# A two-layer hybrid decoder trunk on one core: four plain pairs a feed-forward block instead of five, and other places for operands, squares and bias

## The chip, the core and the metric

The kernel runs on one core of a Trainium2 chip. The core has five engines with an instruction queue each: TensorE (PE, with its weight loads shown as PEld), VectorE (DVE), ScalarE (ACT), GpSimd (POOL) and SyncE (SP), which here only issues DMAs. An engine works through its own instructions in order and waits on semaphores for the others. The metric is the device time of one execution in microseconds; the median of the runs is compared.

## The reference

The input is one sequence of 512 positions with 1024 features. Two layers follow, each a feed-forward block, a mixer of three branches (a state-space scan, attention in a window of 128, a gated unit), and a second feed-forward block. All is in float32.

```
for l in range(DEPTH):
    x = x + 0.5 * swiglu(rmsnorm(x, ffn1_norm[l]), ffn1_w_gate[l], ffn1_w_up[l], ffn1_w_down[l])
    h = rmsnorm(x, mix_norm[l])
    ...
    x = x + jnp.concatenate([y_ssd, y_att, y_sgu], axis=-1) @ w_out[l]
    x = x + 0.5 * swiglu(rmsnorm(x, ffn2_norm[l]), ffn2_w_gate[l], ffn2_w_up[l], ffn2_w_down[l])
return rmsnorm(x, final_norm)

def swiglu(x, w_gate, w_up, w_down):
    return (jax.nn.silu(x @ w_gate) * (x @ w_up)) @ w_down
```

The hidden width of a feed-forward block is 2816, which is 22 chunks of 128. The change touches the two first products of the feed-forward blocks, `x @ w_gate` and `x @ w_up`, the sum of squares of the norms, and the place in which the relative bias of the attention is made.

## The kernel before

The residual x is kept transposed on the chip, as eight tiles `xT` of 128 features by 512 positions. Each float32 product is made of three products in a shorter format: an operand is split into a high part (a cast on ScalarE) and a low part (a subtraction on VectorE), and high times high, low times high and high times low are added up in PSUM. `split` (line 135) does this for a weight tile `raw` of 128x1024 and gives `whi` and `wlo`; `split_x` (line 150) does it for a chunk of x, which it also multiplies with the weight of the norm, and gives `xhi` and `xlo`. `raw` has five buffers, `whi` and `wlo` have four each.

There are four feed-forward blocks; they are called F1 to F4 in order of time here, and between F1 and F2, and between F3 and F4, lies a mixer.

The norm is applied late. `Stat` (line 175) squares the eight chunks on ScalarE and adds the squares up, by default on GpSimd. TensorE adds over the partitions (line 194), VectorE and GpSimd make the reciprocal root, TensorE spreads it (line 207), and VectorE copies it to the tile R (line 371 in a feed-forward block). Products with weights go on meanwhile; only what leaves PSUM is multiplied with R.

A feed-forward block makes its 22 pairs of a gate chunk and an up chunk in two ways. The first `HEAD` pairs (line 42: five) are plain: `in_products` (line 227) runs two tiles of 24 matmuls of 512 columns for each pair, and `emit` (line 354) takes them out of PSUM. A gate tile n (even) is multiplied with R and goes through Silu on ScalarE; an up tile n (odd) is multiplied with it and gives one tile of `h`. Up to three tiles wait for R before the first is taken out.

The other pairs are made by a scheme of seven products of half the size in place of eight (`Seven` and the loop at line 441): sums of weight quarters are multiplied with sums of x quarters, in 84 matmuls of 256 columns. For this x times norm weight times R is needed explicitly, with four sums for each of four pairs of chunks. `operands(c)` (line 335) makes them: two products on VectorE into a temporary (line 343), four sums (lines 346 to 349), then `parts`: one cast of 128x1792 on ScalarE (line 126) and one subtraction on VectorE (line 127). The results are the tiles `as0` to `as3`. The first block of a seven-product pair (line 448) reads all four of them. The temporary is `temp()`, with the tag T and one buffer, so each `operands` waits until line 127 of the one before has read it. The weight sums of a seven-product pair (lines 383 to 386) use the same buffer.

`operands(0)` to `operands(3)` are called in `emit` behind the gate tiles 2, 4, 6 and 8.

In F1 a part of the mixer's work is done too: `attention_bias` (line 97) multiplies the bias table with a one-hot matrix on TensorE (line 106), copies the result to a buffer (line 108) and writes it to DRAM by DMAs of GpSimd's queue (line 109), in four turns over two buffers. It is called when two tiles of `h` are there, and its buffers are parts of one `temp()`.

The code is written in program order; the framework that builds the kernel then orders the instructions of each engine by its own schedule, except where the code asks for the order as written (F1's opening, line 284). The order of the engines shown below is that of the built program.

Of the kernel before, what the change touches and what calls it, by code (L numbers as in the profile page):

```python
# [19 lines left out]
F32 = mybir.dt.float32  # L20
# [6 lines left out]
P = 128  # L27
D = 1024
KD = D // P
T = 512  # L30
# [8 lines left out]

COLS = ("ffn1_norm", "mix_norm", "ffn2_norm", "ssd_norm", "attn_out_norm", "sgu_out_norm", "sgu_ln_w", "conv_b",  # L40
        "conv_w", "d_skip")
HEAD = 5
KEEP = 8
R_F1, R_MX, R_F2, R_SN, R_AN, R_GN, R_LW, R_CB, R_CW, R_DS, N_COL = np.cumsum(
    [0, 16, 16, 16, 8, 4, 4, 4, 16, 64, 8]).tolist()
# [5 lines left out]
def trunk(ctx: ExitStack, tc: tile.TileContext, a: dict, out: bass.AP, phases=None):  # L51
    nc = tc.nc
# [19 lines left out]
    xT = [xp.tile([P, T], F32, name=f"xT{j}") for j in range(KD)]  # L72
# [14 lines left out]
    def vcol(r):  # L87
        return col[:, r:r + 1]
# [8 lines left out]
    def attention_bias(room):  # L97

        relx = rcol("relx")[0:33, :]
        nc.gpsimd.memset(relx, 1.0)  # L100
        nc.sync.dma_start(out=relx[0:32, :], in_=a["rel_bias"])
        ohx = room(0)[0:33, 0:384]
        nc.sync.dma_start(out=ohx, in_=a["onehot"])
        for h in range(4):
            b = bank()
            nc.tensor.matmul(b[:, 0:384], relx[:, h:h + 1].broadcast_to([33, P]), ohx, start=True, stop=True)
            ext = room(1 + h % 2)[:, 0:384]
            nc.vector.tensor_copy(out=ext, in_=b[:, 0:384])
            nc.gpsimd.dma_start(out=skew[h].rearrange("(q i) -> q i", i=385)[:, 0:384], in_=ext)
# [40 lines left out]
    def split_x(src, w):  # L150
        hi, lo = xtile("xhi"), xtile("xlo")
        pinned(nc.scalar.activation(out=hi, in_=src, func=AF.Copy, scale=w))  # L152
        pinned(nc.vector.scalar_tensor_tensor(out=lo, in0=src, scalar=w, in1=hi.bitcast(F32),  # L153
                                              op0=ALU.mult, op1=ALU.subtract))
        return hi, lo
# [55 lines left out]
    def prepare(wrow):  # L211

        st = Stat()
        xs = [split_x(xT[j], vcol(wrow + j)) for j in range(KD)]
        for j in range(KD):
            st.add(xT[j])
        return xs, st

    def prepare_first(wrow, js, xs, st):

        for j in js:
            xs.append(split_x(xT[j], vcol(wrow + j)))
        if js[-1] == KD - 1:
            for j in range(KD):
                st.add(xT[j], nc.gpsimd if j < 4 else nc.vector)

    def in_products(tiles, xs, emit, hooks, levels=None, feed=None, ready=2, lead=3, then=None):

# [42 lines left out]
    def ffn(l, which, first=False, fin=False):  # L271
        gv, uv = (a[f"ffn{which}_w_{s}"][l] for s in ("gate", "up"))
        dv = a["last_w_down" if fin else f"ffn{which}_w_down"]
        wrow = (R_F1 if which == 1 else R_F2) + l * KD
        with tc.tile_pool(name="ff", bufs=1) as ff:
            h = []
# [3 lines left out]
            def temp():  # L280
                return ff.tile([P, 2048], F32, name="tmp", tag="T")

            if first:
# [18 lines left out]
                xs, st = [], Stat()  # L302
                feed = lambda ks: prepare_first(wrow, ks, xs, st)
            else:
                xs, st = prepare(wrow)
# [10 lines left out]
            tiles = []  # L316
            for f in range(HEAD):
                tiles += [maker(gv, f), maker(uv, f)]
# [16 lines left out]
            def operands(c):  # L335
                pair = ff.tile([P, 2, 7, 256], F32R, name=f"as{c}", tag=f"as{c}")
                hi, lo = pair[:, 0], pair[:, 1]
                v = temp()[:, 0:1792].rearrange("p (i n) -> p i n", n=256)
                a11, a12, a22, s1, s2, s3, s4 = (v[:, i, :] for i in range(7))
                a21 = s3  # L340
                tt = nc.vector.tensor_tensor
                for j, o in ((c, v[:, 0:6:5, :]), (c + 4, v[:, 1:3, :])):
                    nc.vector.scalar_tensor_tensor(out=o, in0=xT[j].rearrange("p (s n) -> p s n", s=2),
                                                   scalar=vcol(wrow + j), in1=R.rearrange("p (s n) -> p s n", s=2),
                                                   op0=ALU.mult, op1=ALU.mult)
                tt(out=s1, in0=a21, in1=a22, op=ALU.add)
                tt(out=s3, in0=a11, in1=a21, op=ALU.subtract)
                tt(out=s2, in0=a11, in1=s1, op=ALU.subtract)
                tt(out=s4, in0=a12, in1=s2, op=ALU.add)
                parts(v, hi, lo)  # L350
                lows.append(lo)
                highs.append(hi)

            def emit(n, b):
                if n % 2 == 0:
                    t = ttile32()
                    nc.vector.tensor_tensor(out=t, in0=b, in1=R, op=ALU.mult)
                    nc.scalar.activation(out=t, in_=t, func=AF.Silu)
                    cur[0] = t
                    if n >= 2 and n // 2 <= 4:  # L360
                        operands(n // 2 - 1)
                else:
                    t = cur[0]
                    nc.vector.tensor_tensor(out=t, in0=b, in1=t, op=ALU.mult)
                    nc.vector.scalar_tensor_tensor(out=htile(), in0=t, scalar=0.5, in1=R, op0=ALU.mult, op1=ALU.mult)
                    if first and len(h) == 2:
                        bias = temp()
                        attention_bias(lambda i: bias[:, i * 512:(i + 1) * 512])

            def make():  # L370
                nc.vector.tensor_copy(out=R, in_=st.spread())
# [68 lines left out]
            add = nc.vector.tensor_tensor  # L440
            for f in range(HEAD, KF):
                w, nxt = nxt, Seven(f + 1) if f + 1 < KF else None
# [581 lines left out]
```

## Time and profile before

| | us |
|---|---|
| median of three runs | 1844.29 |
| lowest and highest run | 1844.27, 1846.18 |
| the profiled execution | 1842.94 |
| its span, first to last instruction | 1841.2 |
| TensorE busy | 1810.8 (98%) |
| VectorE busy | 1225.7 (67%) |
| ScalarE busy | 840.4 (46%) |
| GpSimd busy | 130.5 (7%) |
| mean granted TensorE clock | 0.996 |

The span is counted from the first instruction to the last; what lies around it in the profiled execution is 1.7 us. A busy time is the time in which an instruction of the engine was running. Matmuls overlap, so a row's duration (0.39 us for 512 columns) is longer than the distance from one start to the next, and that distance is what a matmul costs in a full stream. On VectorE and ScalarE, too, an instruction's duration reaches a little into the next one. A row of the timeline gives the start, the duration, the engine, the line and operation, the tile that is written and the tiles that are read, and in brackets the idle time ahead of it and what ended this.

### The profile page before, as it was taken

How to read it: one execution, taken by the hardware profiler on the slowest of the kernel's cores; microseconds unless marked ns; L12 is line 12 of the kernel's file. 1: busy time of each engine (PE TensorE's matmuls, PEld its weight loads, DVE VectorE, ACT ScalarE, POOL GpSimd, SP SyncE). 2: the span in 40 equal slices, each digit the busy share in tenths (PEclk: the TensorE clock that was granted, in tenths of full speed). 3: DMA queues.
4: the chain of work that ended last, by engine and by line, in shares of the span. 5: the costliest groups of instructions: out<-in, count | busy, mean ns of one | idle time of the engine just before them, and what ended most of it. 6: DMA issues, size and time to landing. Idle time of an engine off the chain costs nothing.

```text
span 1841.2 us, 27456 instructions
## 1 busy us (share of the span) xinstructions
PE 1810.8 (98%) x11056; PEld 1600.8 (87%) x11056; DVE 1225.7 (67%) x1833; ACT 840.4 (46%) x1278; POOL 130.5 (7%) x126
## 2 busy tenths in 40 slices
PE   8899999999999999999999999999999999999998
PEld 6799998877788899998889999887778888999887
DVE  7788773258865988773368787532887578787422
ACT  5355562238443455562234555432564444555412
POOL 1000001110222000001100000011102210000000
PEclk9899999999999999999999999999999999999999
DMA  5133333351223233333322333323422232333331
GB/s 208 63 104 109 102 111 96 96 154 63 80 71 102 76 108 112 101 109 96 108 94 80 104 104 104 103 93 115 124 89 69 92 91 81 104 104 104 103 102 48
DMA packets 54956, 183.18 MB, mean 99 GB/s; under 512 B 7211, under 2 KB 9196, under 8 KB 54828
## 3 DMA queue, kind: packets, MB, share of 16 engines
q1 hardware_dynamic: 49484, 172.37, 29.5%
q0 software_dynamic: 1920, 6.59, 1.2%
q10 hardware_dynamic: 3424, 2.46, 0.5%
q8 instruction: 87, 1.43, 0.3%
q14 instruction: 41, 0.34, 0.1%
HBM read 178.48 MB, written 2.92 MB: 99 GB/s over the span
## 4 chain that ended last, share of the span: by engine, by line
PE 88%; DVE 7%; ACT 2%; DMA 2%; issue 1%; POOL 0%; POOLq 0%; SPq 0%; ACTq 0%; DVEq 0%
PE accb L163 13%; PE accb L164 13%; PE accb L166 13%; PE accb L419 7%; PE accb L420 7%; PE accb L421 7%; PE mxb L419 5%; PE mxb L421 5%; PE mxb L420 5%; DVE as L127 1%; PE mxb L925 1%; PE mxb L924 1%; PE mxb L923 1%; PE accb L925 1%; PE accb L924 1%
## 5 line engine op out<-in xcount | busy, mean ns | idle before, releaser
L143 ACT CAST whi<-raw 128x1024 fp32r<-128x1024 f32 (+2 forms) x191 | 193.7, 1019 | 478.2 <-PE accb L164 333.5
L144 DVE TENSOR_TENSOR wlo<-raw,whi 128x1024 fp32r<-128x1024 f32 (+2 forms) x191 | 226.7, 1192 | 264.0 <-ACT whi L143 262.9
L163 PE MATMUL accb<-xhi,whi 128*128 128x512 f32 x784 | 310.6, 397 | 6.2 <-ACT xhi L152 6.2
L419 PE MATMUL accb<-as,whi 128*128 128x256 f32 x1088 | 308.8, 284 | 4.2 <-ACT as L126 4.2
L164 PE MATMUL accb<-xlo,whi 128*128 128x512 f32 x784 | 309.4, 395 | 0.5 <-DVE xlo L153 0.5
L420 PE MATMUL accb<-as,whi 128*128 128x256 f32 x1088 | 308.3, 283 | 1.5 <-DVE as L127 1.5
L421 PE MATMUL accb<-as,wlo 128*128 128x256 f32 x1088 | 308.1, 283 | 0.0
L166 PE MATMUL accb<-xhi,wlo 128*128 128x512 f32 x768 | 302.3, 394 | 0.0
L419 PEld LDWEIGHTS accb<-as,whi 128*128 128x128 f32 x1088 | 209.2, 192 | 5.2 <-ACT as L126 4.4
L420 PEld LDWEIGHTS accb<-as,whi 128*128 128x128 f32 x1088 | 209.2, 192 | 2.0 <-DVE as L127 1.8
L421 PEld LDWEIGHTS accb<-as,wlo 128*128 128x128 f32 x1088 | 209.1, 192 | 0.0
L164 PE MATMUL accb<-hp,whi 128*128 128x512 f32 x528 | 205.8, 390 | 0.0
L166 PE MATMUL accb<-hp,wlo 128*128 128x512 f32 x528 | 205.4, 389 | 0.0
L163 PE MATMUL accb<-hp,whi 128*128 128x512 f32 x528 | 205.0, 389 | 0.0
L163 PEld LDWEIGHTS accb<-xhi,whi 128*128 128x128 f32 x784 | 146.6, 187 | 37.6 <-ACT xhi L152 6.4
L164 PEld LDWEIGHTS accb<-xlo,whi 128*128 128x128 f32 x784 | 146.4, 187 | 34.4 <-DVE xlo L153 2.6
L166 PEld LDWEIGHTS accb<-xhi,wlo 128*128 128x128 f32 x768 | 144.9, 189 | 31.1 <-issue 1.6
L399 DVE TENSOR_TENSOR wlo<-tmp,whi 128x1024 fp32r<-128x1024 f32 x136 | 164.8, 1215 | 0.4 <-ACT whi L393 0.4
L419 PE MATMUL mxb<-as,whi 128*128 128x256 f32 x544 | 155.2, 286 | 7.1 <-ACT whi L393 7.1
L187 POOL TENSOR_TENSOR sqs<-sqs,sq 128x512 f32<-128x512 f32 x48 | 78.4, 1634 | 1081.5 <-ACT sq L186 1079.0
L421 PE MATMUL mxb<-as,wlo 128*128 128x256 f32 x544 | 154.7, 284 | 0.0
L420 PE MATMUL mxb<-as,whi 128*128 128x256 f32 x544 | 154.6, 284 | 0.0
(240 smaller groups left out, 3181.8 us busy)
## 6 DMA issues: line engine op xcount, KB each, us to landing
raw<-in_ffn_w_up_dram SPq DMA_DIRECT2D x88, 512.0 KB, 3.6
raw<-in_ffn_w_gate_dram SPq DMA_DIRECT2D x87, 512.0 KB, 3.6
raw<-in_ffn_w_down_dram SPq DMA_DIRECT2D x48, 512.0 KB, 3.5
raw<-in_w_in_dram SPq DMA_DIRECT2D x40, 512.0 KB, 3.6
raw<-in_last_w_down_dram SPq DMA_DIRECT2D x22, 512.0 KB, 3.6
raw<-in_ffn_w_down_dram SPq DMA_DIRECT2D x24, 384.0 KB, 3.1
raw<-in_w_out_dram SPq DMA_DIRECT2D x16, 512.0 KB, 3.5
acb<-arow POOLq DMA_DIRECT2D x8, 512.0 KB, 6.1
```

Source lines behind the costliest of these rows:

```text
L143: pinned(nc.scalar.copy(out=hi[:, c], in_=raw[:, c]))
L144: pinned(nc.vector.tensor_tensor(out=lo[:, c], in0=raw[:, c], in1=hi[:, c].bitcast(F32), op=ALU.subtract))
L163: nc.tensor.matmul(ps, whi[:, i, :], xh, start=(k == first), stop=False)
L164: mm = nc.tensor.matmul(ps, whi[:, i, :], xl, start=False, stop=(wlo is None and k == last))
L166: mm = nc.tensor.matmul(ps, wlo[:, i, :], xh, start=False, stop=(k == last))
L187: eng.tensor_tensor(out=self.s, in0=self.s, in1=q, op=ALU.add)
L399: nc.vector.tensor_tensor(out=lo, in0=self.srcs[i], in1=self.his[i].bitcast(F32), op=ALU.subtract)
L419: nc.tensor.matmul(ps, whi[:, c, :], xh, start=(start and c == 0), stop=False, skip_group_check=True)
L420: nc.tensor.matmul(ps, whi[:, c, :], xl, start=False, stop=False, skip_group_check=True)
L421: mm = nc.tensor.matmul(ps, wlo[:, c, :], xh, start=False, stop=(c == 3), skip_group_check=True)
L924: nc.tensor.matmul(o, hl[:, ts], wh[:, 0, ds], start=False, stop=False)
L925: nc.tensor.matmul(o, hh[:, ts], wl[:, 0, ds], start=False, stop=(f == KF - 1))
```

## The change

`HEAD` is 4 instead of 5, so each of the four feed-forward blocks makes its fifth pair by seven products too, and tiles 8 and 9 of the plain part are gone. The calls of `operands` move: 0 and 1 behind the gate tiles 0 and 2, 2 and 3 behind the up tiles 3 and 5. In F1 the bias is made when three tiles of `h` are there, in the buffers that later hold h5, h6 and h7, and no longer in the temporary. `prepare` and `prepare_first` take the square of each chunk right behind its split, and the last two of seven adds go to VectorE in all blocks; before, `prepare` had all on GpSimd, and `prepare_first` had three on GpSimd and four on VectorE, behind the last split.

```
-HEAD = 5
+HEAD = 4
...
         st = Stat()
-        xs = [split_x(xT[j], vcol(wrow + j)) for j in range(KD)]
+        xs = []
         for j in range(KD):
-            st.add(xT[j])
+            xs.append(split_x(xT[j], vcol(wrow + j)))
+            st.add(xT[j], nc.gpsimd if j < KD - 2 else nc.vector)
...
             xs.append(split_x(xT[j], vcol(wrow + j)))
-        if js[-1] == KD - 1:
-            for j in range(KD):
-                st.add(xT[j], nc.gpsimd if j < 4 else nc.vector)
+            st.add(xT[j], nc.gpsimd if j < KD - 2 else nc.vector)
...
                     cur[0] = t
-                    if n >= 2 and n // 2 <= 4:
-                        operands(n // 2 - 1)
+                    if n == 0 or n == 2:
+                        operands(n // 2)
                 else:
...
-                    if first and len(h) == 2:
-                        bias = temp()
-                        attention_bias(lambda i: bias[:, i * 512:(i + 1) * 512])
+                    if n == 3 or n == 5:
+                        operands(n // 2 + 1)
+                    if first and len(h) == 3:
+                        attention_bias(lambda i: ff.tile([P, T], F32, name="bias", tag=f"h{5 + i}"))
```

In the changed kernel the lines of `emit` and `operands` stand one line higher: 342 is 343 before, 356 is 357, 363 and 364 are 364 and 365. Lines from 371 on are the same.

The order of the engines changes at three places. The first is VectorE in F2, from the third to the fourth set of operands (`t` is the temporary of a plain tile, `tmp` that of the operands, `accb` a PSUM bank with a finished tile). Before:

```order
L127 TENSOR_TENSOR as2_5565<-tmp_5566,as2_5565 128x1792
L365 SCALAR_TENSOR_TENSOR h3_5607<-t_5562,R_5286 128x512
L343 SCALAR_TENSOR_TENSOR tmp_5644<-xT3_78,col_96,R_5286 128x2x256
L343 SCALAR_TENSOR_TENSOR tmp_5644<-xT7_82,col_96,R_5286 128x512
L346 TENSOR_TENSOR tmp_5644<-tmp_5644 128x256
L347 TENSOR_TENSOR tmp_5644<-tmp_5644 128x256
L348 TENSOR_TENSOR tmp_5644<-tmp_5644 128x256
L357 TENSOR_TENSOR t_5640<-accb_5609,R_5286 128x512
L349 TENSOR_TENSOR tmp_5644<-tmp_5644 128x256
L127 TENSOR_TENSOR as3_5643<-tmp_5644,as3_5643 128x1792
L383 TENSOR_TENSOR tmp_5682<-raw_5680,raw_5678 128x512
```

Now:

```order
L127 TENSOR_TENSOR as2_5525<-tmp_5526,as2_5525 128x1792
L363 TENSOR_TENSOR t_5644<-accb_5647,t_5644 128x512
L342 SCALAR_TENSOR_TENSOR tmp_5604<-xT3_78,col_96,R_5348 128x2x256
L342 SCALAR_TENSOR_TENSOR tmp_5604<-xT7_82,col_96,R_5348 128x512
L364 SCALAR_TENSOR_TENSOR h3_5698<-t_5644,R_5348 128x512
L345 TENSOR_TENSOR tmp_5604<-tmp_5604 128x256
L346 TENSOR_TENSOR tmp_5604<-tmp_5604 128x256
L347 TENSOR_TENSOR tmp_5604<-tmp_5604 128x256
L348 TENSOR_TENSOR tmp_5604<-tmp_5604 128x256
L127 TENSOR_TENSOR as3_5603<-tmp_5604,as3_5603 128x1792
L383 TENSOR_TENSOR tmp_5676<-raw_5674,raw_5672 128x512
```

The gate tile 8 is gone from between the sums, and the up tile 7, the last plain tile, is now multiplied ahead of the fourth set's products.

The second place is VectorE in F1, around the copies of the bias (line 108). Before:

```order
L108 COPY tmp_337<-mxb_342 128x384
L108 COPY tmp_337<-mxb_346 128x384
L108 COPY tmp_337<-mxb_350 128x384
L364 TENSOR_TENSOR t_389<-accb_402,t_389 128x512
L108 COPY tmp_337<-mxb_354 128x384
L365 SCALAR_TENSOR_TENSOR h2_434<-t_389,R_122 128x512
L144 TENSOR_TENSOR wlo_542<-raw_539,whi_541 128x1024
L343 SCALAR_TENSOR_TENSOR tmp_393<-xT1_76,col_96,R_122 128x2x256
```

Now:

```order
L363 TENSOR_TENSOR t_388<-accb_391,t_388 128x512
L108 COPY bias_442<-mxb_440 128x384
L364 SCALAR_TENSOR_TENSOR h2_423<-t_388,R_122 128x512
L108 COPY bias_447<-mxb_445 128x384
L127 TENSOR_TENSOR as1_303<-tmp_304,as1_303 128x1792
L108 COPY bias_452<-mxb_450 128x384
L342 SCALAR_TENSOR_TENSOR tmp_348<-xT2_77,col_96,R_122 128x2x256
L342 SCALAR_TENSOR_TENSOR tmp_348<-xT6_81,col_96,R_122 128x512
L108 COPY bias_457<-mxb_455 128x384
```

The second set of operands is now made ahead of and between the copies, and the third set's products start between them; before, the second set's products stood behind all four.

The third place is ScalarE in the opening of F1, where x and the first weights arrive. Before:

```order
L186 ACTIVATE sq_236<-xT4_79 128x512
L186 ACTIVATE sq_239<-xT5_80 128x512
L152 ACTIVATE xhi_179<-xT5_80,col_96 128x512
L186 ACTIVATE sq_242<-xT6_81 128x512
L143 CAST whi_196<-raw_106 128x1024
L152 ACTIVATE xhi_218<-xT6_81,col_96 128x512
L186 ACTIVATE sq_245<-xT7_82 128x512
```

Now:

```order
L186 ACTIVATE sq_189<-xT4_79 128x512
L186 ACTIVATE sq_196<-xT5_80 128x512
L152 ACTIVATE xhi_192<-xT5_80,col_96 128x512
L186 ACTIVATE sq_238<-xT6_81 128x512
L186 ACTIVATE sq_245<-xT7_82 128x512
L143 CAST whi_212<-raw_106 128x1024
L152 ACTIVATE xhi_234<-xT6_81,col_96 128x512
```

The last square stands ahead of the third weight's cast now. The squares have two buffers, so each square from the third on waits for the add two before it; five of the adds are GpSimd's now instead of three.

## Rows read from the trace of the kernel before

**Rows 1.** Windows: stretch, length, busy PE, PEld, DVE, ACT, POOL, clock, DMA

```profile
70.00:90.00 20.00, 12.06 (x72) 11.19 (x71) 15.65 (x23) 8.12 (x11) 0.00 (x0) 0.74 0.17 54
90.00:384.00 294.00, 294.00 (x1938) 270.06 (x1937) 182.91 (x255) 132.35 (x209) 12.38 (x10) 1.00 0.35 106
...
632.00:640.00 8.00, 6.37 (x53) 6.17 (x52) 7.97 (x11) 4.16 (x6) 0.00 (x0) 1.00 0.39 131
```

**Rows 2.** Waits of PE, whole span: total us, times, longest

```profile
PE mxb L419 <- ACT whi L393: 7.1, 4, 2.3
...
PE accb L419 <- ACT as L126: 4.2, 1, 4.2
```

**Rows 3.** Timeline of PE, F2: plain tiles 7 and 8 begin, seven products begin

```profile
615.57 0.39 PE L163 MATMUL accb<-xhi,whi 128*128 128x512 f32 x1
...
621.01 0.39 PE L163 MATMUL accb<-xhi,whi 128*128 128x512 f32 x1
...
631.89 0.28 PE L419 MATMUL accb<-as,whi 128*128 128x256 f32 x1
...
635.11 0.38 PE L419 MATMUL mxb<-as,whi 128*128 128x256 f32 x1 [1.63 <-ACT whi L393]
```

**Rows 4.** Timeline of PE, F1: the seven products begin

```profile
70.37 0.28 PE L419 MATMUL accb<-as,whi 128*128 128x256 f32 x1
...
71.33 0.28 PE L421 MATMUL accb<-as,wlo 128*128 128x256 f32 x1
75.81 0.58 PE L419 MATMUL accb<-as,whi 128*128 128x256 f32 x1 [4.20 <-ACT as L126]
...
80.93 0.58 PE L419 MATMUL mxb<-as,whi 128*128 128x256 f32 x1 [2.26 <-ACT whi L393]
...
81.95 0.41 PE L419 MATMUL mxb<-as,whi 128*128 128x256 f32 x1
...
82.59 0.41 PE L419 MATMUL mxb<-as,whi 128*128 128x256 f32 x1
...
86.00 0.30 PE L420 MATMUL accb<-as,whi 128*128 128x256 f32 x1
```

**Rows 5.** Timeline of DVE, F2, from the first tile taken out

```profile
594.43 1.29 DVE L357 TENSOR_TENSOR t<-accb,R 128x512 f32<-128x512 f32 x2
...
596.90 0.74 DVE L343 SCALAR_TENSOR_TENSOR tmp<-xT,col,R 128x512 f32<-128x512 f32 x1
597.56 0.68 DVE L365 SCALAR_TENSOR_TENSOR h<-t,R 128x512 f32<-128x512 f32 x1
598.16 0.41 DVE L346 TENSOR_TENSOR tmp<-tmp 128x256 f32<-128x256 f32 x1
598.50 1.22 DVE L144 TENSOR_TENSOR wlo<-raw,whi 128x1024 fp32r<-128x1024 f32 x1
599.63 0.41 DVE L347 TENSOR_TENSOR tmp<-tmp 128x256 f32<-128x256 f32 x1
...
610.40 0.69 DVE L364 TENSOR_TENSOR t<-accb,t 128x512 f32<-128x512 f32 x1 [0.17 <-PE accb L166]
...
629.97 2.03 DVE L127 TENSOR_TENSOR as<-tmp,as 128x1792 fp32r<-128x1792 f32 x1 [1.95 <-ACT as L126]
```

**Rows 6.** Timeline of ACT, F2

```profile
599.27 1.06 ACT L143 CAST whi<-raw 128x1024 fp32r<-128x1024 f32 x1 [2.88 <-PE accb L164]
...
628.26 1.68 ACT L126 CAST as<-tmp 128x1792 fp32r<-128x1792 f32 x1
```

**Rows 7.** Timeline of DVE, F1

```profile
11.96 2.30 DVE L144 TENSOR_TENSOR wlo<-raw,whi 128x1024 fp32r<-128x1024 f32 x1
...
53.62 1.42 DVE L343 SCALAR_TENSOR_TENSOR tmp<-xT,col,R 128x512 f32<-128x512 f32 x2 [1.67 <-DMA skew<-tmp]
...
75.78 2.03 DVE L127 TENSOR_TENSOR as<-tmp,as 128x1792 fp32r<-128x1792 f32 x1 [1.75 <-ACT as L126]
```

**Rows 8.** Timeline of POOL, opening of F1

```profile
8.40 4.78 POOL L187 TENSOR_TENSOR sqs<-sqs,sq 128x512 f32<-128x512 f32 x3 [6.78 <-ACT sq L186]
```

## The prediction

> **What bounds the kernel now.** I read the busy time by stretches first, to see where TensorE is not the bound. From 90 to 384 us it is busy for 294.00 of 294 us [rows 1]; the stretches 70 to 90 and 632 to 640 are two of the few holes. Then the waits of TensorE: the largest is for `whi` of line 393, four times, 7.1 us in all, and next to it 4.2 us for `as` of line 126 [rows 2]. Both lie at one place of the program: the step from plain products to seven-product blocks, once in each of the four feed-forward blocks (I call them F1 to F4).
>
> The timeline of TensorE there says what a product costs. In F2 three plain tiles of 24 matmuls run from 615.57 to 631.89 us, so one starts 0.2267 us after the other [rows 3]. The matmuls of 256 columns start 0.120 us apart: eight steps from 70.37 to 71.33 us [rows 4]. A plain pair (48 matmuls) therefore holds TensorE for 10.88 us and a seven-product pair (84 matmuls) for 10.08 us. **A pair turned into seven products saves 0.80 us, and four of them 3.2 us.** That is all that the change can win on TensorE as long as operands are there.
>
> Whether they are is told by VectorE and ScalarE. The seven-product blocks need `as0` to `as3`. All four are made one after the other through the one buffer `tmp`: two products, four sums, a cast on ScalarE, a subtraction on VectorE (line 127). In F2 the last subtraction starts at 629.97 and takes 2.03 us, so it ends at 632.00 [rows 5]; TensorE leaves its last plain tile at 631.89 [rows 3]. The operands are ready at the moment when they are wanted, with nothing to spare. In F1 they are late: TensorE stands from 71.4 to 75.81 us and works in steady flow only from 80.93 us [rows 4].
>
> **The change, part by part.**
>
> *Fifth pair by seven products.* On TensorE minus 0.80 us a block. But TensorE now reaches the seven-product blocks 10.88 us earlier: in F2 at 621.01 us, where today tile 8 starts [rows 3].
>
> *Operands in other places.* What has to be done between R and `as3` on VectorE gets shorter by one emission of a gate (0.60 us) and two `wlo` (1.13 us each), some 2.9 us, not by 10.9. I walk F2 in the new order of VectorE with the start-to-start steps of today's rows [rows 5]: 0.60 us for a 512-wide product or h, 0.66 for one of the two operand products, 0.34 for a 256-wide sum, 1.13 for `wlo`; 2.0 for line 127 and 1.68 for its cast [rows 5, 6]. R and what stands ahead of it keep their places, so the first emission is again at 594.43.
> - `as0`: emission, two products, emission, h, the gate of the next pair and four sums end at 599.5. The cast stands behind the cast of a weight that TensorE frees at 599.27 [rows 6], so it runs from 600.3 to 602.0, and line 127 to 603.9.
> - `as1`: the two products and sums are mixed with two emissions, one `wlo` and `ulo`, and end at 609.5; line 127 stands behind an emission that waits for tile 5, as one does today until 610.40 [rows 5], and an h. It ends at 613.6.
> - `as2`: two products, three sums and a gate emission that needs tile 6 (there at 615.57 + 0.27, the delay seen at tile 5) end at 617.1, the cast at 619.1, line 127 at 621.1.
> - `as3`: ahead of its products now stands the emission of tile 7, there at 621.28. Then products and an h to 623.2 and 623.8, four sums to 625.35, cast 625.4 to 627.1, line 127 to 629.15.
>
> Check on the walk: the sum of the VectorE steps from 594.43 on is 29.7 us, the walk takes 34.7, so it waits 5.0 us. Today's order has 32.5 us of the same steps in 37.6 us, so 5.1 us of waiting. The floor without any wait would be 624.1 us.
>
> After `as3` comes the same tail as today: from the end of line 127 (632.00) to the first block on `mxb` (635.11) 3.1 us, through the sums of the first weights and a cast [rows 3, 5]. So TensorE runs nine matmuls after 621.01, stands from about 622.1, gets a few at 627.1 and 629.15, and flows from 632.26 us. Today it flows from 635.11 us, but with one pair less to come: 632.26 + 10.08 - 635.11 = **7.2 us later in F2**. F3 and F4 have the same order behind R and today the same wait (the four waits of 7.1 us are 2.3 in F1 and 1.6 in each of the others [rows 2]): 21.7 us for the three.
>
> *The clock.* In F1 today, after standing from 71.4 to 75.81, 256-wide matmuls run 0.213 us apart (81.95 to 82.59 for three) instead of 0.120, until 86.00 [rows 4]; the granted clock of that stretch is 0.74, that is a part of it at 1.2 GHz, and 1.00 from 632 to 640, where the stop is short [rows 1]. From 80.93 to 86.00 some 24 matmuls take 5.07 us instead of 2.9: 2.2 us. The new stops in F2 to F4 (5.0, 2.0 and 3.1 us) have the shape of F1's (4.4, 2.1 and 3.1), so I take 2.2 us for each, 6.6 us; the other end is zero, as in today's short stop.
>
> *Bias in h5 to h7, F1.* Today the bias lies in `tmp`, and the products of `as1` wait for its DMAs until 53.62 us; `as3` ends at 77.81 [rows 7]. Free of that, the same walk in F1, begun 0.5 us late (last part below), gives `as1` at 50.6, `as2` at 58.3 and, behind the emission of tile 7 (70.37 - 10.88 + 0.5 + 0.27 = 60.26), `as3` at 66.8, the flow of TensorE at 69.9: 69.9 + 10.08 - 80.93 = -0.95 us. F1 keeps its stop and its slow stretch. Between -3 and +1.5 us is the bound: the first if the emission of tile 7 cost nothing, the second if one copy of the bias waited for its DMA.
>
> *Squares chunk by chunk.* Outside F1 two of seven adds go from GpSimd to VectorE, 0.6 us each, in a stretch in which VectorE waits for `xT` and in which TensorE's statistic stands in the same place of its order (36 matmuls further because F1 has 36 more): nothing. Without that cover it would be 1.2 us a block. In F1 GpSimd gets five adds instead of three, and ScalarE waits for two of them. A `wlo` beside GpSimd's adds takes 2.30 us where 1.22 is usual [rows 5, 7]; three adds take 4.78 us [rows 8]. The earlier first add meets one more half `wlo` (0.68 becomes about 1.3) on the way to TensorE's first chunks: +0.5 us, which is in the walk of F1. The bounds are 0 and 1.5 us.
>
> The Trainium skill (page "SBUF — State Buffer", section "Who interferes with whom") says that a VectorE instruction with two SBUF inputs and a GpSimd instruction that reads SBUF exclude each other for the whole instruction. The 2.30 us agree with it in kind. By that rule the two added adds of 1.6 us could hold VectorE for 3.2 us, and the sum below would be 30 instead of 27.3.
>
> The Trainium skill (page "TensorE: Matmul & The Clock Gate", section "Back-to-back issue gap") gives an isolated gap of N / 2.4 + 2.5 ns, so 109 and 216 ns here. By that estimate a pair would save 1.2 us instead of 0.8, and the sum would be 25.7. The rows show 120 and 226.7 ns, and they decide.
>
> **Sum.** 3 x (7.2 + 2.2) - 0.95 = +27.3 us. The profiled execution took 1842.94 us (span 1841.2); the median of the runs is 1844.29, 1.35 us above it. I set the sum on the median: 1871.6, **forecast 1871.5 us**.
>
> **The rivals.**
> 1. *The operands are late, but the clock is not cut.* The stops are broken by a few matmuls. For it: no row shows a stop of this length in F2 to F4. Against it: F1's stops are broken in the same way. 1871.5 - 6.6 = 1865 us.
> 2. *The chain is longer than walked.* VectorE waits in order, so each emission that waits for a tile holds the next operand behind it, and ScalarE's casts do likewise; 3 us more in each of F2 to F4 give 1880 us.
> 3. *The operands are in time; not slower.* The place is the end of `as3` in F2 to F4. Breakeven is `as3` at 621.9 us, 7.2 us before my walk. It needs R some 7 us earlier, as it would be if the statistic, whose squares are now added as the chunks arrive, were also taken on TensorE as soon as they are complete. Then four pairs save 0.80 us and the short stops stay: 1844.3 - 3.2 = 1841 us. Against it stands that the statistic keeps its place in the order, and that VectorE's own work from R alone ends at 624.1.
>
> **How the numbers follow.** The forecast has 0.62, its own range is 1864 to 1879. Rival 1 has 0.15, rival 2 has 0.13, rival 3 has 0.05; 0.05 is left for what I don't see. A measurement of this kernel can tell about 0.2% (3.7 us) from no change. Rival 3 lies at 3.2 us below and counts partly as no change: faster 0.04, same 0.03, slower 0.93. The range has to take in rival 1 with a little less lateness and rival 2: 1857 to 1882.
>
> **What would show it.** In the changed kernel TensorE should wait for `as` of line 126 in all four blocks, 4 to 5 us each in F2 to F4, then about 2 us for line 127 and 3 us for `whi` of line 393; the granted clock in the 10 us behind should fall below 1 in F2 to F4. The 84 matmuls of a pair should take 10.1 us. The subtraction of `as1` in F1 should end near 50.6 us, before its products even begin today (53.62). I am wrong if line 127 of `as3` ends within 1 us of TensorE's last plain tile in F2 to F4, or if R stands some 7 us earlier against the plain tiles.

## The result, and the profile after

The changed kernel takes 1870.37 us (median of four runs, 1868.72 to 1871.52) where the kernel before takes 1844.28: a ratio of 1.0140, 95% interval 1.0128 to 1.0152, or 26.1 us more. The forecast was 1871.5. The profiled execution of the changed kernel took 1868.72 us, its span is 1867.0.

The waits of TensorE in the whole span (total us, times, longest), the answer to [rows 2]:

```profile
PE accb L419 <- ACT as L126: 18.6, 4, 5.0
PE mxb L419 <- ACT whi L393: 9.1, 4, 2.3
...
PE accb L420 <- DVE as L127: 5.9, 4, 1.5
```

TensorE now waits for the operands in all four blocks, and for longer: 18.6 + 9.1 + 5.9 = 33.6 us, against 4.2 + 7.1 + 1.5 = 12.8 us before ([rows 2] and this line of the same view):

```profile
PE accb L420 <- DVE as L127: 1.5, 1, 1.5
```

Where before only F1 had the three waits one after the other [rows 4], each block has them now. F2 on TensorE, against [rows 3]:

```profile
620.02 0.28 PE L419 MATMUL accb<-as,whi 128*128 128x256 f32 x1
...
626.27 0.58 PE L419 MATMUL accb<-as,whi 128*128 128x256 f32 x1 [5.01 <-ACT as L126]
628.33 0.58 PE L420 MATMUL accb<-as,whi 128*128 128x256 f32 x1 [1.48 <-DVE as L127]
...
631.38 0.58 PE L419 MATMUL mxb<-as,whi 128*128 128x256 f32 x1 [2.26 <-ACT whi L393]
...
632.41 0.41 PE L419 MATMUL mxb<-as,whi 128*128 128x256 f32 x1
...
634.50 0.28 PE L421 MATMUL mxb<-as,wlo 128*128 128x256 f32 x1
...
637.13 0.28 PE L419 MATMUL mxb<-as,uhi 128*128 128x256 f32 x1
```

The plain tiles end at 620.02, nine matmuls run, and then TensorE stands. From 631.38 it flows, but at first a matmul starts 0.21 us after the other, and 0.12 us only from 634.50 on. Two stretches of [rows 1] show the clock (windows; the columns are as there):

```profile
90.00:384.00 294.00, 294.00 (x1938) 270.09 (x1938) 181.91 (x255) 132.05 (x209) 9.31 (x8) 1.00 0.35 105
...
620.00:640.00 20.00, 11.25 (x73) 10.43 (x72) 16.52 (x24) 8.57 (x11) 0.00 (x0) 0.74 0.20 60
```

Far from the step nothing has changed (294.00 busy of 294 us). In 620 to 640 TensorE is busy for 11.25 of 20 us and the granted clock is 0.74 (a part at 1.2 GHz, the rest at 2.4), where it was 1.00 before. VectorE in F2, against [rows 5]:

```profile
618.36 2.03 DVE L127 TENSOR_TENSOR as<-tmp,as 128x1792 fp32r<-128x1792 f32 x1 [1.95 <-ACT as L126]
...
626.25 2.02 DVE L127 TENSOR_TENSOR as<-tmp,as 128x1792 fp32r<-128x1792 f32 x1 [1.75 <-ACT as L126]
```

The fourth set is ready at 628.27, 8.25 us after the last plain tile. In F1 the second set's subtraction is at 49.06 us, no longer behind the bias's DMAs [rows 7], but the plain tiles end at 60.41 and the fourth set at 67.20:

```profile
49.06 2.01 DVE L127 TENSOR_TENSOR as<-tmp,as 128x1792 fp32r<-128x1792 f32 x1
...
65.18 2.02 DVE L127 TENSOR_TENSOR as<-tmp,as 128x1792 fp32r<-128x1792 f32 x1 [1.75 <-ACT as L126]
```

How the loss is spread over the program is read from the matmuls of the statistic, which stand in the same place of every block (TensorE, F2 to F4). Before:

```profile
587.85 0.95 PE L194 MATMUL mxb<-ones,sqs 128*128 128x1 f32 x8
...
937.53 0.95 PE L194 MATMUL mxb<-ones,sqs 128*128 128x1 f32 x8
...
1490.07 0.95 PE L194 MATMUL mxb<-ones,sqs 128*128 128x1 f32 x8
```

After:

```profile
586.87 0.95 PE L194 MATMUL mxb<-ones,sqs 128*128 128x1 f32 x8
...
944.96 0.95 PE L194 MATMUL mxb<-ones,sqs 128*128 128x1 f32 x8
...
1506.60 0.95 PE L194 MATMUL mxb<-ones,sqs 128*128 128x1 f32 x8
```

The difference is -0.98 us at F2, +7.43 at F3, +16.53 at F4 and +25.8 at the end of the span. So F1 and the first mixer gain 1.0 us, and F2, F3 (with the second mixer) and F4 lose 8.4, 9.1 and 9.3 us.

### The profile page after: what moved, and what is told of

The parts are those of the page before. It is cut to its first block, busy times and chain, and to the rows that moved or that the text cites. A ratio compares the mean times of both kernels' runs of the same rounds, so it can differ in the third digit from the quotient of the medians.

```text
span 1867.0 us, 27791 instructions
## 1 busy us (share of the span) xinstructions
PE 1813.9 (97%) x11200; PEld 1610.2 (86%) x11200; DVE 1246.1 (67%) x1869; ACT 850.2 (46%) x1302; POOL 117.9 (6%) x118
## 4 chain that ended last, share of the span: by engine, by line
PE 89%; DVE 6%; ACT 1%; DMA 1%; issue 1%; POOL 0%; SPq 0%; POOLq 0%; ACTq 0%; DVEq 0%
PE accb L163 13%; PE accb L164 13%; PE accb L166 13%; PE accb L420 7%; PE accb L419 7%; PE accb L421 7%; PE mxb L419 6%; PE mxb L420 6%; PE mxb L421 6%; DVE as L127 1%; PE mxb L923 1%; PE mxb L925 1%; PE mxb L924 1%; PE accb L923 1%; PE accb L925 1%; PE accb L924 1%
## 5 line engine op out<-in xcount | busy, mean ns | idle before, releaser
L419 PE MATMUL accb<-as,whi 128*128 128x256 f32 x1152 | 328.2, 285 | 18.6 <-ACT as L126 18.6
L420 PE MATMUL accb<-as,whi 128*128 128x256 f32 x1152 | 328.1, 285 | 5.9 <-DVE as L127 5.9
L421 PE MATMUL accb<-as,wlo 128*128 128x256 f32 x1152 | 327.0, 284 | 0.0
L163 PE MATMUL accb<-xhi,whi 128*128 128x512 f32 x720 | 285.5, 397 | 6.3 <-ACT xhi L152 6.3
L164 PE MATMUL accb<-xlo,whi 128*128 128x512 f32 x720 | 284.0, 394 | 1.5 <-DVE xlo L153 1.5
L166 PE MATMUL accb<-xhi,wlo 128*128 128x512 f32 x704 | 277.3, 394 | 0.8 <-DVE wlo L144 0.8
L419 PEld LDWEIGHTS accb<-as,whi 128*128 128x128 f32 x1152 | 222.4, 193 | 19.7 <-ACT as L126 19.4
L420 PEld LDWEIGHTS accb<-as,whi 128*128 128x128 f32 x1152 | 222.3, 193 | 7.4 <-DVE as L127 7.1
L421 PEld LDWEIGHTS accb<-as,wlo 128*128 128x128 f32 x1152 | 222.0, 193 | 0.0
L419 PE MATMUL mxb<-as,whi 128*128 128x256 f32 x576 | 167.0, 290 | 9.1 <-ACT whi L393 9.1
L420 PE MATMUL mxb<-as,whi 128*128 128x256 f32 x576 | 165.7, 288 | 0.0
L399 DVE TENSOR_TENSOR wlo<-raw,whi 128x1024 fp32r<-128x1024 f32 x72 | 88.2, 1225 | 113.2 <-ACT whi L393 113.2
L393 ACT CAST whi<-tmp 128x1024 fp32r<-128x1024 f32 x144 | 151.0, 1051 | 18.3 <-ACT t L433 10.3
```

Of the source, the lines that this page charges most:

```text
L163: nc.tensor.matmul(ps, whi[:, i, :], xh, start=(k == first), stop=False)
L164: mm = nc.tensor.matmul(ps, whi[:, i, :], xl, start=False, stop=(wlo is None and k == last))
L166: mm = nc.tensor.matmul(ps, wlo[:, i, :], xh, start=False, stop=(k == last))
L393: nc.scalar.copy(out=hi, in_=self.srcs[i])
L399: nc.vector.tensor_tensor(out=lo, in0=self.srcs[i], in1=self.his[i].bitcast(F32), op=ALU.subtract)
L419: nc.tensor.matmul(ps, whi[:, c, :], xh, start=(start and c == 0), stop=False, skip_group_check=True)
```

## The experiments

The theory: what costs the time is the fourth set of operands, which is late since the plain tiles end 10.9 us earlier. The rivals: that another part of the change (places, bias, squares) costs time by itself; that R comes too late rather than that the sets follow each other too slowly; and that the slow stretch behind the stop is not the clock's. All times are medians, beside the kernel before on the same chip.

| run | median, us | ratio to before, 95% interval |
|---|---|---|
| bias_only | 1834.42 | 0.9951 (0.9934 to 0.9967) |
| places_only | 1844.39 | 1.0002 (0.9992 to 1.0011) |
| squares_only | 1846.05 | 1.0010 (1.0001 to 1.0019) |
| head5 | 1833.39 | 0.9942 (0.9927 to 0.9957) |
| filler | 1870.91 | 1.0143 (1.0128 to 1.0158) |
| filler2 | 1864.60 | 1.0105 (1.0090 to 1.0120) |
| two_temps | 1832.74 | 0.9933 (0.9916 to 0.9949) |
| stat_early | 1853.12 | 1.0046 (1.0031 to 1.0061) |
| best0 | 1825.14 | 0.9893 (0.9878 to 0.9908) |
| best0_five | 1827.53 | 0.9907 (0.9892 to 0.9922) |
| best1 | 1826.72 | 0.9900 (0.9883 to 0.9916) |
| best0_squares | 1825.97 | 0.9895 (0.9880 to 0.9910) |

The runs were made on three chips, on which the kernel before took 1843.8, 1844.9 and 1845.9 us, so a difference of one or two microseconds between the medians of two rows can be the chip's.

### The parts of the change apart

**head5**, the changed kernel with the old number of plain pairs:

```
-HEAD = 4
+HEAD = 5
```

> The changed kernel with five plain pairs; all else of the change stays. Theory (the loss is the fourth set of operands, which comes 5 to 7 us after the last plain tile): with 10.9 us more of plain tiles the set is there in time in all four blocks. In F1 the stop and the slow clock go (about 10 us), in F2 to F4 today's stop of 1.8 us in front of the mxb blocks goes (5 us): about 1829 us. Rival (the new places, the bias or the squares cost time by themselves): not under 1844 us.

Measured: 1833.39 us, 10 us faster than before and 37 us faster than the changed kernel. So the one line `HEAD` costs 37 us, and the rest of the change together gains 10. The stops of F2 to F4 did not go, though; in F2 TensorE leaves the last plain tile at 621.89 and waits 1.41 us:

```profile
624.89 0.39 PE L419 MATMUL mxb<-as,whi 128*128 128x256 f32 x1 [1.41 <-ACT whi L393]
```

Before it was 1.63 us [rows 3]. Nearly all of the gain is F1's: the statistic of F2 stands at 577.85 us instead of 587.85.

**bias_only**, the kernel before with one edit:

```
-                    if first and len(h) == 2:
-                        bias = temp()
-                        attention_bias(lambda i: bias[:, i * 512:(i + 1) * 512])
+                    if first and len(h) == 3:
+                        attention_bias(lambda i: ff.tile([P, T], F32, name="bias", tag=f"h{5 + i}"))
```

> The kernel before with one edit: the bias in h5 to h7 when three tiles of h are there. Theory: the second set in F1 no longer waits for the bias's DMAs (until 53.62 us before), the fourth ends near 68 us instead of 77.8, before the plain tiles end at 70.4; the stop of F1 and its slow clock go, F2 to F4 are as before: 1834 us. Rival (VectorE's copies wait for the DMAs in the same way wherever the buffers are): 1842 to 1845 us.

Measured: 1834.42 us, as the theory had it. VectorE in F1:

```profile
49.18 2.02 DVE L127 TENSOR_TENSOR as<-tmp,as 128x1792 fp32r<-128x1792 f32 x1
...
52.50 0.56 DVE L108 COPY bias<-mxb 128x384 f32<-128x384 f32 x1 [0.83 <-DMA skew<-bias]
...
67.37 2.03 DVE L127 TENSOR_TENSOR as<-tmp,as 128x1792 fp32r<-128x1792 f32 x1 [1.16 <-ACT as L126]
```

One copy still waits 0.83 us for a DMA, but no set of operands does. The fourth is ready at 69.40 us, before the plain tiles end, and TensorE's only stop at F1's step is 0.84 us. This edit alone brings 9.4 of the 10.4 us that head5 gains.

**places_only**, the kernel before with one edit:

```
-                    if n >= 2 and n // 2 <= 4:
-                        operands(n // 2 - 1)
+                    if n == 0 or n == 2:
+                        operands(n // 2)
...
+                    if n == 3 or n == 5:
+                        operands(n // 2 + 1)
```

> The kernel before with one edit: operands at the gate tiles 0 and 2 and the up tiles 3 and 5; five plain pairs. Theory: in F2 to F4 the fourth set is ready some 2 us before the last plain tile ends and the stop of 1.8 us goes in each (5 us); in F1 the bias in the temporary still holds one set, and the stop stays within 2 us of before: 1839 us, 1837 to 1842. Rival (the places alone cost time): over 1844.3 us.

Measured: 1844.39 us, no change; the theory's 5 us did not come. VectorE and TensorE in F2:

```profile
621.88 2.03 DVE L127 TENSOR_TENSOR as<-tmp,as 128x1792 fp32r<-128x1792 f32 x1 [1.76 <-ACT as L126]
...
630.44 2.03 DVE L127 TENSOR_TENSOR as<-tmp,as 128x1792 fp32r<-128x1792 f32 x1 [1.95 <-ACT as L126]
```

```profile
635.59 0.38 PE L421 MATMUL mxb<-as,whi 128*128 128x256 f32 x1 [1.41 <-ACT whi L395]
```

The fourth set is ready at 632.47; here the statistic stands at 588.56, so that is 43.9 us behind it, against 44.2 before (632.00 and 587.85). The sets are called earlier but made at nearly the same time. What sets their distance is not the place of the call; two_temps below shows what does.

**squares_only**, the kernel before with the new `prepare` and `prepare_first`:

```
+            st.add(xT[j], nc.gpsimd if j < KD - 2 else nc.vector)
```

> The kernel before with one edit: the squares chunk by chunk. Theory: TensorE's opening of F1 loses 0.9 us to GpSimd's five adds beside VectorE (statistic at 25.6 instead of 24.7), the other blocks lose nothing: 1845.2 us. Rival A (the two adds on VectorE are paid in every block and mixer): 1849 us. Rival B (the 0.9 us vanish in the stop of F1, which ends with the bias's DMAs): 1844.3 us.

Measured: 1846.05 us, by its interval 0.2 to 3.5 us slower than before. TensorE's statistic in F1 is at 26.07 us instead of 24.66:

```profile
26.07 0.95 PE L194 MATMUL mxb<-ones,sqs 128*128 128x1 f32 x8
```

That is 1.4 us, more than the theory's 0.9 and less than rival A's. From F2's statistic to F3's the run takes 349.67 us where the kernel before takes 349.68, so behind F1 nothing is paid for the adds in a feed-forward block, as the theory had it. In the opening the loss begins at half a `wlo` on VectorE (line 144, 128x512). Before, it starts at 7.98 us and takes 0.68 us; now it starts at 8.39 and takes 1.42 us, and one of GpSimd's adds runs beside it, from 7.93 to 9.26 us. TensorE then waits 1.57 us for the `xlo` behind it, where it waited 0.49. The price is measured once more with best0_squares, below.

### The clock

**filler**, the changed kernel with 21 matmuls behind the last plain tile:

```
+            def filler():
+                w = seven(HEAD)
+                b = bank()
+                for i in range(21):
+                    mm = nc.tensor.matmul(b, xs[0][0][:, 0:P], xs[i % KD][0], start=True, stop=True,
+                                          skip_group_check=True)
...
-                              then=lambda: seven(HEAD))
+                              then=filler)
```

> The changed kernel with 21 more matmuls of 512 columns (4.76 us, into a bank that nobody reads) right behind the last plain tile of each feed-forward block; nothing that the operands wait for is touched. Theory (the slow matmuls behind the new stop are the clock, which falls because TensorE stood): the granted clock stays at 1.00 in 620 to 640 us, the matmuls on mxb run 0.12 us apart from the first one, and 1.9, 1.3, 1.5 and 2.2 us come back in F1 to F4: 6.9 us, 1863.5. Rival (the slow stretch has another cause, as operands that come slowly): 1870 us or, if the fillers push the rest back, more.

Measured: 1870.91 us, nothing came back. TensorE in F2, and the stretch 620 to 640 us:

```profile
620.39 4.92 PE L441 MATMUL mxb<-xhi 128*128 128x512 f32 x21
...
626.64 0.38 PE L419 MATMUL accb<-as,whi 128*128 128x256 f32 x1 [0.25 <-ACT as L126]
628.70 0.48 PE L420 MATMUL accb<-as,whi 128*128 128x256 f32 x1 [1.68 <-DVE as L127]
631.76 0.58 PE L419 MATMUL mxb<-as,whi 128*128 128x256 f32 x1 [2.37 <-ACT whi L393]
...
634.91 0.41 PE L421 MATMUL mxb<-as,wlo 128*128 128x256 f32 x1
```

```profile
620.00:640.00 20.00, 15.70 (x90) 14.12 (x89) 16.15 (x24) 7.83 (x10) 0.00 (x0) 0.83 0.16 52
```

The long wait is filled, and the clock (0.83) falls all the same, only later. This leaves two readings: that the two waits left, 1.68 and 2.37 us, are enough to lose it, or that the slow stretch has another cause.

**filler2** fills most of these two as well:

```
+                    if c == 3 and fills:
+                        fill(fills[0])
...
+                block(x, w.part(0), A11, True, True, (6,) if f == HEAD else ())
+                if f == HEAD:
+                    fill(9)
```

> The run filler with more matmuls: 21 behind the last plain tile, and in the first seven-product pair of each block some 6 to 9 in the wait for line 127 of the fourth set and some 5 to 9 in the wait for the first weight sums (all of 512 columns into a bank that nobody reads). Theory (the clock falls on the waits of 1.7 and 2.4 us that were left in filler): now the granted clock stays at 1.00 in 620 to 640 us, the matmuls on mxb run 0.12 us apart from the first on, and the 1.9, 1.3, 1.5 and 2.2 us of F1 to F4 come back: 1863.5 us. Rival (the slow stretch is not the clock's): 1869 us or more, since the operands come no earlier.

Measured: 1864.60 us. TensorE in F2, and the same stretch:

```profile
631.84 0.38 PE L419 MATMUL mxb<-as,whi 128*128 128x256 f32 x1 [1.26 <-ACT whi L393]
632.06 0.28 PE L422 MATMUL mxb<-as,whi 128*128 128x256 f32 x1
```

```profile
620.00:640.00 20.00, 18.71 (x119) 16.53 (x118) 17.63 (x25) 8.55 (x11) 0.00 (x0) 1.00 0.20 63
```

The operands come as late as before (631.84 against 631.38), and still the matmuls start 0.12 us apart at once and the granted clock is 1.00. The slow stretch is the clock's, then, and TensorE's standing still is its cause. From the first matmul on mxb to the first on `uhi` the four blocks of the changed kernel take 6.31, 5.75, 5.88 and 6.57 us, and those of filler2 4.41 us each: the clock is worth 6.9 us by the traces. The medians, from two batches of runs, give 5.8 us (1870.4 less 1864.6).

### What holds the fourth set back

**two_temps**, the changed kernel with a second buffer for the temporary; `KEEP` pays for it, as two more tiles of h lie in another pool. Not shown are two edits that follow from it: the bias lies in h3, h4 and a `t`, and the last product of the block (`room`) takes its space from both buffers:

```
-KEEP = 8
+KEEP = 6
...
-                return ff.tile([P, 2048], F32, name="tmp", tag="T")
+                return ff.tile([P, 2048], F32, name="tmp", tag="T", bufs=2)
```

> The changed kernel with two buffers for the temporary of the operands (two of h's buffers are given up for it, the bias lies in h3, h4 and a t). Theory (the operand sets come about 7.8 us apart because each waits for line 127 of the one before, through the one temporary): the sets come closer, the fourth ends near 622.5 us in F2 instead of 628.3, the weight sums no longer wait for it, TensorE flows from about 623 instead of 631.4 and the clock stays up: some 34 us less, 1836 us. Rival (VectorE's work and the emissions, not the buffer, set the distance): the fourth set moves by under 2 us, 1862 us or more.

Measured: 1832.74 us, 38 us less than the changed kernel, with the same number of pairs and the same places of the calls. VectorE and TensorE in F2:

```profile
593.57 2.02 DVE L127 TENSOR_TENSOR as<-tmp,as 128x1792 fp32r<-128x1792 f32 x1
...
612.59 0.68 DVE L386 TENSOR_TENSOR tmp<-raw,tmp 128x512 f32<-128x512 f32 x1
...
614.33 2.02 DVE L127 TENSOR_TENSOR as<-tmp,as 128x1792 fp32r<-128x1792 f32 x1
```

```profile
612.62 0.28 PE L419 MATMUL accb<-as,whi 128*128 128x256 f32 x1
...
614.19 0.39 PE L419 MATMUL mxb<-as,whi 128*128 128x256 f32 x1 [1.18 <-ACT whi L393]
```

From the first subtraction to the fourth it is 20.8 us, where the changed kernel takes 25.3 (600.97 to 626.25). Neither these two nor those at 599.97 and 606.91 have idle time ahead of them now: VectorE makes the sums of the next set while ScalarE casts. And the weight sums of the seven-product pair, which share the tag, no longer wait for the fourth set, so the tail of 3.1 us behind it is gone as well: the last of them (line 386) stands ahead of the fourth subtraction, and TensorE flows 1.57 us after the last plain tile instead of 11.4.

The fourth set itself is still late: it ends at 616.35 us, 3.7 us after the last plain tile (8.25 in the changed kernel). TensorE has work in that time, the products on mxb, because the weight sums are there. So the one buffer costs twice: in the distance of the sets, and in holding back the weight sums. From the statistic to the first `uhi` matmul the four blocks take 7.8, 9.4, 9.5 and 10.3 us less than in the changed kernel, 37.0 together, so nearly all of the 38 us are won at the steps and not by this run's other edits elsewhere.

**stat_early**, the changed kernel with an earlier R in F2 to F4, as in the prediction's third rival:

```
-{(3, 1) if first else (1, 0): st.start, (3 if first else 1, "R"): make}
+{(3, 1): st.start, (3, "R"): make} if first else {(0, 1): st.start, (0, 2): make}
```

> The changed kernel, where in F2 to F4 TensorE adds up the squares behind the first plain tile's first six chunks and spreads R behind the second's (before: behind all three). This is the rival of the prediction in which R comes some 7 us earlier. Theory (the distance from R to the fourth set is what is too long): R comes 7 us earlier, VectorE makes the first set before a tile is complete, the fourth ends near 617 us in F2, before the plain tiles end at 620; the stops of F2 to F4 go and 33 to 36 us with them: 1836 us. F1 is as in the changed kernel. Rival (the sets behind the first wait for the tiles that are emitted between them, so the gain is lost on the way): over 1850 us.

Measured: 1853.12 us, half of what the theory had. VectorE and TensorE in F2:

```profile
587.18 0.69 DVE L371 COPY R<-mxb 128x512 f32<-128x512 f32 x1 [4.31 <-PE mxb L207]
...
593.26 2.02 DVE L127 TENSOR_TENSOR as<-tmp,as 128x1792 fp32r<-128x1792 f32 x1
...
622.21 2.03 DVE L127 TENSOR_TENSOR as<-tmp,as 128x1792 fp32r<-128x1792 f32 x1 [1.76 <-ACT as L126]
```

```profile
624.29 0.38 PE L420 MATMUL accb<-as,whi 128*128 128x256 f32 x1 [0.56 <-DVE as L127]
627.82 0.38 PE L419 MATMUL mxb<-as,whi 128*128 128x256 f32 x1 [3.03 <-ACT whi L393]
```

The plain tiles end at 622.37 here, 34.5 us after R; in the changed kernel it is 26.6 us. R is thus 7.9 us earlier, and the fourth set ends 1.9 us after the plain tiles instead of 8.25: 6.4 of the 7.9 us arrive. But its temporary is free only then, so the weight sums and the 3.03 us behind them remain, and in the stretch behind the clock falls again (0.91):

```profile
620.00:640.00 20.00, 16.41 (x113) 15.57 (x112) 16.99 (x23) 9.35 (x13) 0.00 (x0) 0.91 0.28 82
```

An early R brings 17 us, but it does not undo what follows from one temporary.

### Versions that beat both kernels

**best0** has two temporaries, the early R, the bias as changed, F1's squares as before, and a number of plain pairs for each block:

```
+            HEAD = 5 if first else 4
```

> Five plain pairs in F1, four in F2 to F4, two temporaries, the early R of F2 to F4, F1's squares as in the kernel before. Theory: no stop is left at the step to seven products in any block. From five pairs with stops of 1.4 us in three blocks (1833.4 us): less 4.2 for the stops, 2.4 for three pairs, 1 for the squares: 1826 us. Rival (VectorE has no room for it, stops stay): 1831 us or more.

Measured: 1825.14 us, 1.07% faster than before. Of TensorE's waits (whole span) none at the step to seven products is left:

```profile
PE accb L162 <- ACT xhi L151: 5.9, 1, 5.9
PE mxb L781 <- DVE s L778: 1.9, 2, 1.0
```

VectorE has no room left there: at the step of F2 it is busy for all of the 20 us, with TensorE (window of best0):

```profile
608.00:628.00 20.00, 20.00 (x155) 19.41 (x155) 20.00 (x28) 9.66 (x16) 0.00 (x0) 1.00 0.36 110
```

**best0_five** is best0 with `HEAD = 5` in all blocks.

> best0 with five plain pairs in all four blocks. Theory (without stops a plain pair costs 10.88 us and a seven-product pair 10.08): three pairs at 0.80 us more than best0's 1825.1: 1827.5 us. Rival (the fifth pair by seven products gains nothing, as the work of VectorE on its weights costs it elsewhere): 1825 us or less.

Measured: 1827.53 us, as expected, though its interval and best0's overlap. The traces say it without that noise, from the first `uhi` matmul of F2 to that of F3, between which no mixer lies. best0, then best0_five:

```profile
616.98 0.28 PE L421 MATMUL mxb<-as,uhi 128*128 128x256 f32 x1
...
963.68 0.28 PE L421 MATMUL mxb<-as,uhi 128*128 128x256 f32 x1
```

```profile
627.22 0.28 PE L421 MATMUL mxb<-as,uhi 128*128 128x256 f32 x1
...
974.74 0.28 PE L421 MATMUL mxb<-as,uhi 128*128 128x256 f32 x1
```

346.70 against 347.52 us: one pair by seven products is worth 0.82 us, when nothing waits.

**best1** is best0 with `HEAD = 4` in F1 too.

> best0 with four plain pairs in F1 too. Theory (in F1 x comes from memory, R is there at 31 us, and four sets through two temporaries end later than 59.5 us, where the plain tiles would): stops of some 2 us against a saving of 0.8: 1826.5 us. Rival (two temporaries are enough in F1 as well): 1824.3 us.

Measured: 1826.72 us. TensorE waits 0.93 us in F1's plain tiles (best0: 0.57) and 1.18 at the step (best0: none), more than the pair saves: the fifth pair's first `uhi` matmul stands at 76.75 us in best0, and at 77.92 here. The medians do not show it; their difference is within the intervals.

**best0_squares** is best0 with F1's squares chunk by chunk.

> best0 with F1's squares chunk by chunk as in the changed kernel. Theory (GpSimd's five adds beside VectorE delay the opening): TensorE's statistic in F1 0.9 to 1.4 us later and as much in the end: 1826.0 to 1826.5 us. Rival: nothing, 1825.1 us.

Measured: 1825.97 us. TensorE's statistic in F1 stands at 25.76 us instead of best0's 24.40: the opening loses 1.4 us. At the first `uhi` matmul of F1 1.05 us of it are left (77.80 against 76.75). The medians, 0.8 us apart, are too close to show it.

## Why the prediction was right, point by point

- **Lateness of the fourth set.** The walk had the sets of F2 end at 603.9, 613.6, 621.1 and 629.15 us. With the 0.98 us by which F2 stands earlier, that is 602.9, 612.6, 620.1 and 628.2; measured are 602.99, 612.77, 620.39 and 628.27. The flow was forecast 7.2 us later in each block. Counted from the statistic it starts at 44.51 us (631.38 - 586.87) instead of 47.26, with 10.08 us more to come: 7.3 us.
- **The clock.** The mechanism was right, and filler2 shows it. The size was not: 2.2 us were put for each of F2 to F4. From the first matmul on mxb to the first on `uhi` it takes 4.41 us at full clock (bias_only, filler2) and 5.75, 5.88 and 6.57 us in the changed kernel: 1.3, 1.5 and 2.2 us, 5.0 instead of 6.6 us. This term is why the forecast lies above the measured 1870.4. That F1's price would carry over was taken from one row group. Nearly the same three waits (5.0, 1.5 and 2.3 us) cost 1.3, 1.5 and 2.2 us in F2 to F4, and no run shows what sets the price between them; a closer forecast of this term would have been luck.
- **F1.** Forecast -0.95 us, measured -0.98 at F2's statistic. The parts differ a little: the flow started at 70.3 instead of 69.9, as the statistic came 0.4 us later than put down for the squares, and the clock cost 1.9 instead of 2.2. bias_only shows what the bias edit is worth when the tiles are there to cover the sets: 9.4 us. In the changed kernel the missing pair takes all of it but 1 us.
- **Squares.** Forecast +0.5 us in F1 with bounds of 0 and 1.5. In the changed kernel's own trace the statistic of F1 is 0.9 us later (25.57 against 24.66). Over all traces it stands at 24.39 to 24.66 us in the six with the old squares and at 25.40 to 26.45 in the eight with the new ones, 1.4 us later on average: mis-sized, inside its bounds. The place was right: half a `wlo` takes 1.42 us (squares_only), where about 1.3 was put down. The Trainium skill (page "SBUF — State Buffer", section "Who interferes with whom") would, by the prediction's estimate from it, have VectorE held for 3.2 us by the two adds. The runs agree that there is a price and show less than half of that at TensorE's statistic.
- **The saving.** 0.80 us a pair was forecast, 0.82 measured with best0 and best0_five. The Trainium skill's isolated gap (page "TensorE: Matmul & The Clock Gate", section "Back-to-back issue gap") would, as an estimate, have made it 1.2 us; the measured 0.82 us does not agree with it.
- **The rivals.** Rival 1 (clock not cut) fell: 0.74 in the stretch. Rival 2 (3 us more per chain) did not come. Rival 3's condition, R 7 us earlier, was built as stat_early and did not bring 1841 but 1853 us. Its price does not fit its own breakeven: with the fourth set at 621.9 us, 0.9 us after the last plain tile, the flow starts at 625.0 and the time only stays as it is; 1841 us needs the set 0.8 us earlier still. It also left out two things: that part of an earlier R is lost on the way (6.4 of 7.9 us arrived, and the set ended 1.9 us after the last plain tile), and that two shorter stops in a row still lower the clock (5.89 instead of 4.41 us from the first matmul on mxb to the first on `uhi` in F2). From F2's first `uhi` to F3's stat_early takes 352.30 us and the kernel before 349.67.
- **What the prediction did not see.** It put down 2.9 us less from R to the fourth set, and counted from the statistic it is 41.4 instead of 44.15 us: 2.75 less. That is the work of the missing pair, as it said; the new places, under which it stood, bring 0.2 us (places_only). It named the single temporary in its first part, but gave it no price and no rival of its own, and two_temps shows that the buffer was worth 38 us. It also tied TensorE's flow to the end of the fourth set: in two_temps the set ends 3.7 us after the last plain tile, well past the breakeven of 0.9 us, and TensorE waits only 1.18 us. The sum came out right all the same, since the walk followed the order row by row and so contained the buffer's waits.

## What to carry to other kernels

Before taking work off the engine that sets the pace, ask what that work was covering: here 10.9 us of plain tiles hid the making of four operand sets, and a saving of 0.8 us a block cost 9. Where sets are made through one buffer, count the buffer's round trip (write, cast on another engine, subtract) and not the work, and ask who else uses the tag. Moving a call up in the program did nothing here while its buffer was not free.

## What the runs showed of the hardware

The granted clock of TensorE fell on shorter stops than the one of 5 us, too. Single stops of 1.63 us (before), 1.41 (head5) and 1.26 (filler2) left the granted clock at 1.00. Two stops of 1.68 and 2.37 us with few matmuls between them (filler), or 0.56 and 3.03 (stat_early), brought it to 0.83 and 0.91 in 620 to 640 us, with matmuls of 256 columns 0.21 us apart instead of 0.12 for some 4 us of F2. How the length of one stop and the work between two stops trade against each other was not tried.

A subtraction of 128x512 on VectorE that takes 0.68 us in the kernel before took 1.42 us in squares_only, where an add of GpSimd had begun ahead of it.
